# Moving one load to another queue, a block of vector work ahead of another, and eight more zero products, in the pool layer of a two-layer transformer with mixture of experts

## The chip, the cores and the metric

The kernel runs on one core of one Trainium2 chip. The metric is the device time of one execution in microseconds (us), as the median of several runs. One further execution is taken by the hardware profiler; all rows below are of that one execution, with times in us from the start of its span.

## The reference, cut to what matters

Two layers work on 512 tokens of width 1024. The first mixes the tokens by attention, the second by pooling; each is followed by a mixture of experts with 32 experts, of which every token takes two. Before each part the tokens are normed and modulated with a scale and a shift that come from a conditioning vector and the matrix `w_ada` (the modulation). The change lies around the pooling of the second layer:

```python
def pool_mixer(h, w_pool, scale):
    cs = concatenate([0, cumsum(h, axis=1)])
    for gi, win in enumerate((2, 4, 8, 16)):
        lo, hi = maximum(t - win // 2, 0), minimum(t + win // 2, n)
        mean = (cg[:, hi] - cg[:, lo]) / (hi - lo)
        diff = mean - h[..., sl]
        outs.append(diff @ w_pool[gi])
    return concatenate(outs, axis=-1) * scale

x = x + g_m * pool_mixer(modulate(rms_norm(x), sh_m, sc_m))
tokens = modulate(rms_norm(x), sh_f, sc_f)
x = x + g_f * hierarchical_moe(tokens, router weights, w_gate_up, w_down)
```

The router takes a softmax over four groups and the best two of the eight experts in the best group.

## The kernel before, in words

**Weights.** All large weights go through one stream: `plan_stream` lists them in the order of use, `Stream.fill` (the load itself is L136) issues loads on SyncE's queue while fewer than `limit` tiles are out, and `Stream.done` is called when a tile has been used and refills. In the expert layers twelve tiles of 1 MB are out (`RING`). One pair of experts takes eight tiles of gate/up and four of down weights, twelve in all. The last pair's tiles of layer 1 come as two loads of 512 KB each, and so do the gate/up tiles of the first pair of layer 2. Between the layers eight tiles of modulation weights (`ada(1, 2)`, 1 MB each) stand in the stream: in order down weights of pair 15, eight modulation tiles, gate/up weights of the next layer's pair 0. Loads on one queue are issued in the order of the program.

**The experts.** `moe` runs over 16 pairs. For each it multiplies gate and up weights (`up`), adds the previous pair's results (`combine`), gathers the tokens of the next group (`gather`, every second pair works on the same group of four experts), and multiplies the down weights. At the pairs 13 and 14 it takes a step of `late`, a generator that prepares what the next layer needs: `prepare_pool` loads router and pool weights at the first step and scales them at the second. The gathers read a one-hot matrix `OH`, a tile with one buffer; the last of them in a layer comes in pair 13.

**The last pair and the pool layer.** `last_down` multiplies the down weights in two halves of 512 columns. Each half goes through `y`: VectorE gates the product, ScalarE writes the rounded part of `y` (L1410), VectorE the rest (L1450), then TensorE scatters it (`pc`, L1456), VectorE adds it to `x` (L1459) and ScalarE squares the sum (L1460). Between the products of the second half and its `y`, `gap` is called: `pool_begin`. It allocates a new `OH` tile, whose space is used for the banded matrices (`bands`), loads these on ScalarE's queue (L1672), and multiplies the first two modulation tiles (L371). `pool_layer` multiplies four more modulation tiles on TensorE, makes the normed tokens `xn` (L1659, L1661), transposes them (L1700), and treats the eight chunks of 128 columns in two ways: chunks 4 to 7 (windows 8 and 16) by products with the bands (`means`, L1742), chunks 0 to 3 by shifted sums on VectorE (`summed`, L1722 to L1732). The last two modulation tiles stand between (`ada_parts(2)`). `project` multiplies the pool weights (L1759) into the banks g, u, t and y, `added` adds the result to `x` (L1771) and squares it (L1774). `router` multiplies the router weights with the modulation (L1141, L1147) and reads the result with VectorE (L1150 to L1154). `turn` transposes `x` (L1784), `logits` multiplies the router (L1791), and `choose` finds the experts on VectorE (L1181 to L1235). Meanwhile TensorE multiplies zeros into the four banks of the next gather (`zeros`, L1341); these products also clear the banks. Then come `rank` (L1244), the gather itself (L1349) and the second expert layer.

On every engine the instructions run in the order of the program.

Of the kernel before, what the change touches and what calls it, by code (L numbers as in the profile page):

```python
# [11 lines left out]
F32 = mybir.dt.float32  # L12
F32R = mybir.dt.float32r
# [10 lines left out]
NT = SEQ // 128  # L24
# [11 lines left out]
NPAIR = NE // 2  # L36
NWR = (KD - 1) * (NG + NE) + 128

CAP = 56
# [27 lines left out]
_C = {}  # L67
# [129 lines left out]
class Kernel:  # L197
# [1365 lines left out]
    def moe(self, i, late, first, then=lambda: None, later=iter(()), gap=lambda: None):  # L1563

        nc, st = self.nc, self.st
        gf = self.fw[:, 0]
        xe, OH = {0: first}, {}

        def gather(g, k):

            if k == 0:
                xe[g] = self.slots_tile()
            self.gather(i, k, OH[g], 4 * CAP, xe[g][:, k, :4 * CAP])

        self.overflow(i, gf)
        early = self.slots()
        st.fill(RING + 2)
        hold, comb = {}, []

        def up_weights(p, k):  # L1580
            if p in ENDS:
                t = st.get()
                return t[:, 0], t[:, 1]
            if k % 2 == 0:
                hold[0] = [st.get(), st.get()]
            return hold[0][0][:, k % 2], hold[0][1][:, k % 2]

        def down_weights(k):
            if k % 2 == 0:
                hold[0] = [st.get(), st.get()]  # L1590
            return hold[0][0][:, k % 2], hold[0][1][:, k % 2]

        def used(p, k):
            if p == 0:
                next(early, None)
                if k in (4, 6):
                    next(later, None)
            if p in ENDS:
                st.done()
            elif k % 2:  # L1600
                st.done(2)


        st.limit -= 2
        for p in range(NPAIR):
            g = p // 2
            if p % 2 == 0 and p + 2 < NPAIR:
                OH[g + 1] = self.one_hot(g + 1)
            act = self.up(lambda k: xe[g][:, k], [(p % 2 * 2 + e) * CAP for e in range(2)], lambda k: up_weights(p, k), after=lambda k: used(p, k))
            for _ in early:  # L1610
                pass

            turns = [lambda k=k: gather(g + 1, k) for k in range(p % 2 * 4, p % 2 * 4 + 4)] if g + 1 < NPAIR // 2 else []
            for n in range(3):
                for unit in comb[2 * n:2 * n + 2]:
                    unit()
                if turns:
                    turns.pop(0)()
            if turns:
                for unit in comb[6:]:  # L1620
                    unit()
            aT = self.turn_act(act)
            for unit in turns or comb[6:]:
                unit()
            if p in (NPAIR - 3, NPAIR - 2):
                next(late, None)
            w, inv = self.sw[:, p:p + 1], self.sinv[:, p:p + 1]
            if p == NPAIR - 1:

                nc.scalar.activation(self.sm.tile([128, 1], F32, name="warm", bufs=1), self.rk[:, 0, 0:1], AF.Sqrt)  # L1630
                return self.last_down(aT, w, gf, inv, then, gap)
            y = self.down(aT, down_weights, w, gf, lambda k: k % 2 and st.done(2))
            P = self.scatter(inv)
            comb = [unit for h in range(2) for unit in self.combine(P, y[h], h)]


    def prepare_pool(self):

        nc, a = self.nc, self.a
        gw = self.gw = self.big([128, 2, D], F32, "gw")  # L1640
        pw = self.pw = self.big([128, 8, 256], F32, "pw")
        nc.sync.dma_start(gw[:, 1, :NWR], a["w_router"][1])
        self.row_load("pool_scale", lambda h: gw[32 * h:32 * h + 1, 0, :512])
        nc.sync.dma_start(pw, a["pool_w"].rearrange("g (k p) n -> p (g k) n", p=128))
        yield
        for h in range(2):
            row = self.gates[32 * h:32 * h + 1]
            nc.gpsimd.tensor_tensor(row, row, gw[32 * h:32 * h + 1, 0, :512], op=ALU.mult)
        self.row_bcast(self.bank, 2, gw[:, 0])
        for g in range(4):  # L1650
            nc.gpsimd.tensor_tensor(pw[:, 2 * g:2 * g + 2], pw[:, 2 * g:2 * g + 2],
                                    gw[:, 0, None, g * 256:(g + 1) * 256].to_broadcast([128, 2, 256]), op=ALU.mult)

    def scaled(self, norms, outs):

        nc = self.nc
        for j, r in norms:
            if j % 2:
                nc.scalar.activation(outs[j], self.x(j), AF.Copy, scale=r)  # L1659
            else:  # L1660
                nc.vector.tensor_scalar(outs[j], self.x(j), r, 0.0, op0=ALU.mult, op1=ALU.add)  # L1661
# [5 lines left out]

    def pool_begin(self):

        self.bands = self.mp.tile([128, NT, 4 * CAP], F32R, name="OH").rearrange("p a b -> p (a b)").bitcast(F32)  # L1670
        a, b = _C["band"]
        self.nc.scalar.dma_start(self.bands[:, :b - a], self.a["consts"][:, a:b])  # L1672
        self.ada_begin(self.pm, 1, 2, "ga")
        self.ada_parts(2)

    def pool_layer(self, norms):
        nc, mp, pm, st, sm, pw = self.nc, self.mp, self.pm, self.st, self.sm, self.pw
# [39 lines left out]
        def summed(k):  # L1717

            eng = nc.vector
            g = k // 2  # L1720
            h, c, other = (ab[k][:, z] for z in range(3))
            eng.tensor_tensor(c[:, 1:], h[:, 1:], h[:, :-1], op=ALU.add)  # L1722
            w, lo, hi = 2, 1, SEQ + 2 * PAD
            while w < WINDOWS[g]:
                o = w // 2
                eng.tensor_tensor(other[:, lo + o:hi - o], c[:, lo:hi - 2 * o], c[:, lo + 2 * o:hi], op=ALU.add)
                c, other, w, lo, hi = other, c, 2 * w, lo + o, hi - o
            for e, t0 in ((0, PAD), (8, PAD + SEQ - 8)):
                eng.tensor_tensor(c[:, t0:t0 + 8], c[:, t0:t0 + 8], self.edge[:, 16 * g + e:16 * g + e + 8], op=ALU.mult)
            q = slice(PAD, PAD + SEQ)  # L1730
            diff[k] = other[:, q]
            eng.scalar_tensor_tensor(diff[k], c[:, q], 1.0 / WINDOWS[g], h[:, q], op0=ALU.mult, op1=ALU.subtract)  # L1732
# [19 lines left out]
        def project(g, tags):  # L1752

            ps = []
            for jj in range(2):
                p = pm.tile([128, 2, 256], F32, tag=tags[jj], name="pp")
                for j in range(2):
                    for z in range(2):
                        nc.tensor.matmul(p[:, j], diff[2 * g + z][:, (2 * jj + j) * 128:(2 * jj + j + 1) * 128],  # L1759
                                         pw[:, 2 * g + z], start=(z == 0), stop=(z == 1))  # L1760
                ps.append(p)
            return g, ps
# [3 lines left out]
        def added(g, ps):  # L1766

            q = slice(g * 256, (g + 1) * 256)
            for jj in range(2):
                xs = self.xt[jj][:, :, q]  # L1770
                nc.vector.tensor_add(xs, xs, ps[jj])  # L1771
                for j in (2 * jj, 2 * jj + 1):
                    junk = mp.tile([128, 256], F32, name="act")
                    nc.scalar.activation(junk, self.x(j)[:, q], AF.Square, accum_out=ss[:, j, g:g + 1])  # L1774
# [46 lines left out]
        padded(3)  # L1821
        added(*p0)
        p3 = project(3, ("g", "u"))
        self.router(1, self.gw[:, 1])
        self.norm_begin()
        nc.tensor.matmul(self.lg, *zero, start=True, stop=False)
        summed(2)
        summed(3)
        p2 = project(2, ("t", "y"))
        added(*p3)  # L1830
        turn(0, "c", nc.scalar)
# [37 lines left out]
            high(j)  # L1869
        self.banks = {}  # L1870
        for k, tag in ((0, "g"), (2, "u"), (4, "c"), (6, "c")):
            self.zeros(k, tag, 3)
        self.rank(range(NT))
        OH = mp.tile([128, NT, 4 * CAP], F32R, name="OH")
        for j in range(2):
# [81 lines left out]
```

## Time and profile before

| what | value |
|---|---|
| median of the runs | 1393.6 us (1393.39 to 1394.07, three runs) |
| the profiled execution: its time | 1395.2 us |
| its span, first to last instruction | 1393.4 us |
| its mean granted TensorE clock | 0.981 |
| TensorE busy over the span | 95% |
| bytes read from HBM | 472.51 MB, 341 GB/s over the span |

How to read it: engines are PE (TensorE), DVE (VectorE), ACT (ScalarE), POOL (GpSimd) and SP (SyncE). A "q" behind the name is the engine's sequencer, which waits and issues loads. "out<-in" names the tile written and the tiles read. In square brackets stands how long the engine was idle before the instruction and what ended most of that; with a wait for several things it is the one that came last by the profile. Rows of the timeline merge equal instructions that follow each other. The granted clock is 1.00 at 2.4 GHz and 0.50 at 1.2 GHz.

### The profile page before, as it was taken

To read this page: it belongs to the slowest core of one execution; us is meant where nothing else is said; L and a number is where in the kernel's file an instruction comes from. 1 tells how busy PE (TensorE), PEld (TensorE's weight loads), DVE (VectorE), ACT (ScalarE), POOL (GpSimd) and SP (SyncE) were. 2 spreads that over 40 slices of the span, in tenths; PEclk is the share of its full clock that TensorE was granted. 3 is DMA by queue.
4 is the path that set the end of the run, shared out by engine and by line. 5 is a ranking of instruction groups with operands and counts; after the bars stand their busy time and mean duration, and the time that the engine had idled before them with its cause. 6 is when DMAs were issued, how large, how long until landed. Compare 5 with 4: busy or idle time off the path is not lost. (4 is left out here: it accounts for less than half of the span.)

```text
span 1393.4 us, 18658 instructions
## 1 busy us (share of the span) xinstructions
PE 1318.3 (95%) x7179; PEld 738.4 (53%) x7183; DVE 659.7 (47%) x1290; ACT 364.1 (26%) x707; POOL 130.8 (9%) x130
## 2 busy tenths in 40 slices
PE   4799999999899999999999996989999999999995
PEld 1578677778645444554445433854445544454442
DVE  2778788767814343343334334552433433343325
ACT  2554687763311110111111114521101111111103
POOL 0523343340000000000000100000000000000001
PEclk8799999999999999999999998999999999999998
DMA  9411836159499999999999999259999999999994
GB/s 374 164 61 61 343 141 212 52 197 388 195 363 427 426 427 425 427 427 426 427 426 427 414 411 410 118 221 407 426 426 427 426 426 427 426 426 426 427 420 179
DMA packets 80704, 475.91 MB, mean 342 GB/s; under 512 B 8512, under 2 KB 10064, under 8 KB 30432
## 3 DMA queue, kind: packets, MB, share of 16 engines
q1 hardware_dynamic: 80456, 474.22, 83.0%
q8 instruction: 58, 0.95, 0.3%
q10 hardware_dynamic: 152, 0.42, 0.1%
q14 instruction: 38, 0.31, 0.1%
HBM read 472.51 MB, written 2.11 MB: 341 GB/s over the span
## 5 line engine op out<-in xcount | busy, mean ns | idle before, releaser
L1371 PE MATMUL pgate<-wt,xe 128*64 128x512 f32 x1024 | 272.7, 593 | 3.5 <-ACTq L1504 2.1
L1371 PE MATMUL pup<-wt,xe 128*64 128x512 f32 x1024 | 271.3, 592 | 0.3 <-DVEq L1504 0.3
L1396 PE MATMUL py<-wt,aT 128*64 128x512 f32 x960 | 212.6, 595 | 0.0
L1376 DVE TENSOR_TENSOR act<-act,pup 128x512 f32<-128x512 f32 x32 | 22.0, 688 | 343.7 <-ACT act L1375 309.8
L1427 DVE TENSOR_TENSOR x<-x,pc 128x512 f32<-128x512 f32 x240 | 153.9, 683 | 29.9 <-PE pc L1425 29.9
L1371 PEld LDWEIGHTS pgate<-wt,xe 128*64 128x64 f32 x1024 | 75.8, 137 | 149.0 <-issue 128.5
L1371 PEld LDWEIGHTS pup<-wt,xe 128*64 128x64 f32 x1024 | 76.7, 137 | 145.0 <-issue 142.1
L1425 PE MATMUL pc<-y,scat 128*128 128x512 f32 x480 | 136.6, 406 | 2.3 <-DVE x L1427 2.3
L1409 DVE SCALAR_TENSOR_TENSOR py<-py,r_sw,gw 128x512 f32<-128x512 f32 x64 | 48.5, 758 | 178.4 <-PE py L1396 169.5
L1396 PEld LDWEIGHTS py<-wt,aT 128*64 128x64 f32 x960 | 66.9, 137 | 124.0 <-issue 118.8
L1325 PE MATMUL pga<-OH,xnp 128*128 128x224 f32 x896 | 119.3, 277 | 0.0
L1325 PEld LDWEIGHTS pga<-OH,xnp 128*128 128x128 f32 x896 | 114.3, 191 | 8.5 <-issue 1.6
L1375 ACT ACTIVATE act<-pgate 128x512 f32<-128x512 f32 x32 | 19.1, 597 | 361.5 <-PE pgate L1371 349.3
L1425 PEld LDWEIGHTS pc<-y,scat 128*128 128x128 f32 x480 | 80.3, 189 | 42.8 <-ACT act L1375 24.3
L1410 ACT ACTIVATE y<-py 128x512 fp32r<-128x512 f32 x64 | 38.2, 597 | 247.4 <-PE py L1396 182.0
L1334 POOL MEMSET xe<- 128x64 f32 x16 | 2.4, 152 | 785.0 <-PE pup L1371 610.0
L1360 ACT ACTIVATE xe<-pga,mod 128x224 f32<-128x224 f32 x64 | 33.9, 539 | 156.4 <-PE pga L1325 137.2
L562 PE MATMUL pmm<-whl,hT 128*128 128x512 f32 x288 | 70.3, 401 | 0.0
L850 DVE TENSOR_REDUCE mx<-S 128x1 f32<-128x768 f32 x64 | 58.2, 951 | 19.6 <-PE S L847 18.9
L562 PEld LDWEIGHTS pmm<-whl,hT 128*128 128x128 f32 x288 | 54.3, 192 | 11.3
L857 ACT ACTIVATE P<-S,mx 128x768 f32<-128x768 f32 x64 | 57.0, 900 | 2.2 <-POOL rest L731 2.1
L867 PE MATMUL PT<-cst,P 128*128 128x128 f32 x384 | 54.5, 278 | 0.1
(344 smaller groups left out, 1420.9 us busy)
## 6 DMA issues: line engine op xcount, KB each, us to landing
wt<-in_moe_w_gate_up_dram SPq DMA_DIRECT2D x224, 1024.0 KB
wt<-in_moe_w_down_dram SPq DMA_DIRECT2D x120, 1024.0 KB
wt<-in_w_ada_dram SPq DMA_DIRECT2D x48, 1024.0 KB
wt<-in_moe_w_gate_up_dram SPq DMA_DIRECT2D x64, 512.0 KB
wt<-in_moe_w_down_dram SPq DMA_DIRECT2D x16, 512.0 KB
wt<-in_attn_w_qkv_dram SPq DMA_DIRECT2D x6, 1024.0 KB
x<-in_x_dram SPq DMA_DIRECT2D x8, 512.0 KB
wt<-in_attn_w_o_dram SPq DMA_DIRECT2D x4, 1024.0 KB
```

The lines of the kernel that those rows point to most:

```text
L562: self.nc.tensor.matmul(p, lhs(pa, k), whl[pb, k // 4][:, k % 4], start=(k + n == 0), stop=(k == KD - 1 and n == 2))
L850: nc.vector.tensor_reduce(m, s[:, :NKEY], axis=AX, op=ALU.max, negate=True)
L857: nc.scalar.activation(P[n][:, g], S.pop((n, g))[:, :NKEY], AF.Exp, bias=mx[n, g], accum_out=total[n // 4][:, 2 * gp + g, kvl:kvl + 1])
L867: nc.tensor.transpose(pt[:, cc, g * 128:(g + 1) * 128], P[n][:, g, c * 128:(c + 1) * 128], self.ident)
L1325: nc.tensor.matmul(p[:, :n], self.parts[part][j // 2][:, j % 2, k * 128:(k + 1) * 128], OH[:, j], start=(z == 0), stop=(z == 2 * NT - 1))
L1360: nc.scalar.activation(xe, p, AF.Identity, bias=B[:, k:k + 1], scale=A[:, k:k + 1])
L1371: nc.tensor.matmul(p[64 * e:64 * e + 64], xe(k)[:, offs[e]:offs[e] + UNIT], w[e][:, h * 512:(h + 1) * 512], start=(k == 0), stop=(k == KD ...
L1396: nc.tensor.matmul(py[h][64 * e:64 * e + 64], aT[:, j, 64 * e:64 * e + 64], wd[e][:, h * 512:(h + 1) * 512], start=(j == 0), stop=(j == 3) ...
L1409: nc.vector.scalar_tensor_tensor(py, py, w, gf[:, h * 512:(h + 1) * 512], op0=ALU.mult, op1=ALU.mult)
L1410: nc.scalar.activation(y[:, 0], py, AF.Copy)
L1425: nc.tensor.matmul(p, P[:, j * 128:(j + 1) * 128], y[:, part], start=(part == 0), stop=(part == 1))
L1427: nc.vector.tensor_add(xs, xs, p)
```

## The change

Three edits, all between the last pair of experts of layer 1 and the first pair of layer 2.

1. The load of the banded matrices leaves `pool_begin` and ScalarE's queue. It becomes a third step of `prepare_pool`, taken at the start of pair 15, on SyncE's queue. At that point of the program all twelve tiles of pair 15 are listed before it, and the modulation tiles come after it.
2. In `pool_layer` the shifted sums of chunks 2 and 3 stand ahead of the router's work instead of behind it.
3. `zeros` multiplies five products instead of three into each of the four banks.

```diff
@@ moe, in the loop over the pairs
+            if p == NPAIR - 1:
+                next(late, None)
             act = self.up(...)
@@ prepare_pool, at its end
+        yield
+
+        self.bands = self.mp.tile([128, NT, 4 * CAP], F32R, name="OH").rearrange("p a b -> p (a b)").bitcast(F32)
+        u, v = _C["band"]
+        nc.sync.dma_start(self.bands[:, :v - u], a["consts"][:, u:v])
@@ pool_begin
-        self.bands = self.mp.tile([128, NT, 4 * CAP], F32R, name="OH").rearrange("p a b -> p (a b)").bitcast(F32)
-        a, b = _C["band"]
-        self.nc.scalar.dma_start(self.bands[:, :b - a], self.a["consts"][:, a:b])
         self.ada_begin(self.pm, 1, 2, "ga")
         self.ada_parts(2)
@@ pool_layer
         added(*p0)
         p3 = project(3, ("g", "u"))
+        summed(2)
+        summed(3)
         self.router(1, self.gw[:, 1])
         self.norm_begin()
         nc.tensor.matmul(self.lg, *zero, start=True, stop=False)
-        summed(2)
-        summed(3)
         p2 = project(2, ("t", "y"))
@@ pool_layer, after the choice has been issued
-            self.zeros(k, tag, 3)
+            self.zeros(k, tag, 5)
```

## Rows read from the trace of the kernel before

**Rows 1.** The page, the span in 40 equal slices of 34.8 us: GB/s moved

```profile
GB/s 374 164 61 61 343 141 212 52 197 388 195 363 427 426 427 425 427 427 426 427 426 427 414 411 410 118 221 407 426 426 427 426 426 427 426 426 426 427 420 179
```

**Rows 2.** Windows: length, busy us of each engine, granted clock, DMA share, GB/s

```profile
853.00:859.00 6.00, 5.57 (x20) 3.03 (x24) 3.39 (x7) 2.57 (x8) 0.00 (x0) 0.50 1.03 419
885.00:890.00 5.00, 3.42 (x20) 2.90 (x19) 4.81 (x10) 1.69 (x7) 0.00 (x0) 1.00 0.01 3
911.00:914.00 3.00, 3.00 (x16) 3.00 (x16) 3.00 (x7) 0.00 (x0) 0.00 (x0) 0.50 0.03 8
915.00:918.00 3.00, 3.00 (x30) 3.00 (x28) 0.00 (x0) 0.03 (x1) 0.00 (x0) 1.00 0.00 0
925.00:1375.00 450.00, 447.78 (x2278) 213.28 (x2275) 162.73 (x284) 54.18 (x93) 1.06 (x7) 1.00 1.00 418
```

**Rows 3.** Timeline of ScalarE: start, length, instruction, idle before and its releaser

```profile
834.57 0.60 ACT L1410 ACTIVATE y<-py 128x512 fp32r<-128x512 f32 x1 [3.43 <-DVE py L1409]
...
840.32 0.19 ACT L1460 ACTIVATION_READ_ACCUMULATOR act<-x 128x1 f32 x1
852.17 0.36 ACTq L1672 DMA_DIRECT2D OH<-in_consts_dram  x1
852.78 0.60 ACT L1410 ACTIVATE y<-py 128x512 fp32r<-128x512 f32 x1 [12.28 <-DMA wt<-in_moe_w_gate_up_dram]
...
860.27 1.13 ACT L1659 ACTIVATE xn<-x,nr 128x1024 f32<-128x1024 f32 x1
```

**Rows 4.** Timeline of TensorE, 835 to 868

```profile
835.32 2.13 PE L1456 MATMUL pc<-y,scat 128*128 128x512 f32 x8
...
839.24 1.92 PE L371 MATMUL ada_ps<-wt,cond 128*32 128x512 f32 x16
...
853.43 3.78 PE L1456 MATMUL pc<-y,scat 128*128 128x512 f32 x8 [12.26 <-ACT y L1410]
...
861.82 2.17 PE L1700 MATMUL pt<-cst,xn 128*128 128x128 f32 x16
...
866.26 1.92 PE L371 MATMUL ada_ps<-wt,cond 128*32 128x512 f32 x16
```

**Rows 5.** Loads of L136 on SyncE's queue: count, ns to issue, first and last start; timeline

```profile
L136 SPq DMA_DIRECT2D wt<-in_w_ada_dram x8: 327/328/668, 823.6 to 832.6; - x8
...
L136 SPq DMA_DIRECT2D wt<-in_moe_w_gate_up_dram x7: 327/328/328, 835.0 to 849.8; - x7
...
847.30 0.33 SPq L136 DMA_DIRECT2D wt<-in_moe_w_gate_up_dram  x1
```

**Rows 6.** Readers of the tile `OH`, 760 to 870: ns each, first and last start

```profile
L1325 PE MATMUL pga<-OH,xnp x32: 266/274/352, 762.4 to 769.1; 128*128 128x224 f32 x32
...
L1742 PE MATMUL pm<-OH,xn x23: 276/279/286, 864.0 to 869.9; 128*128 128x143 f32 x8, 128*128 128x135 f32 x8, 128*128 128x136 f32 x4, 128*128 128x132 f32 x2
```

**Rows 7.** Timeline of VectorE, 877 to 890

```profile
877.79 1.27 DVE L1771 TENSOR_TENSOR x<-x,pp 128x512 f32<-128x512 f32 x2
882.09 0.17 DVE L1150 COPY mod<-pb 128x16 f32<-128x16 f32 x1 [3.03 <-PE pb L1147]
...
882.65 0.72 DVE L1722 TENSOR_TENSOR pab<-pab 128x543 f32<-128x543 f32 x1
...
887.45 2.47 DVE L1771 TENSOR_TENSOR x<-x,pp 128x512 f32<-128x512 f32 x4
```

**Rows 8.** Timeline of TensorE, 885 to 890

```profile
885.66 1.04 PE L1784 MATMUL pb<-cst,x 128*128 128x128 f32 x8
888.27 1.97 PE L1759 MATMUL pp<-pw,pab 128*128 128x256 f32 x8 [1.58 <-DVE x L1771]
```

**Rows 9.** Timeline of TensorE, 902 to 920

```profile
903.50 2.57 PE L1341 MATMUL pga<-ones_b,tri_b 128*128 128x512 bf16 x11
908.89 0.18 PE L1244 MATMUL pr<-r_M,tri_b 128*128 128x32 bf16 x1 [2.82 <-DVE r_M L1235]
...
910.19 9.08 PE L1349 MATMUL pga<-OH,xnp 128*128 128x224 f32 x64 [0.27 <-DVE OH L1553]
```

## The prediction

> **What bounds the kernel now.** I read the page's 40 slices first. In most slices the weights flow at 426 or 427 GB/s; around the pool layer (slices 25 to 27) they fall to 410, 118 and 221 [rows 1]. The twelve weight tiles that may be out are loaded there and the queue has nothing to do until the second expert layer frees one. What the pool layer takes is therefore paid in full. Behind it TensorE is busy 447.8 of 450 us while the weights run at 418 GB/s [rows 2]: both are full there, but both start from the same event, the first product of the second expert layer, so whatever the pool layer gives back shifts that stretch as a whole.
>
> Next the timeline engine by engine. ScalarE ends its squares at 840.32 + 0.19 = 840.51 and does nothing until 852.17, when it issues the bands' load; at 852.78 comes `y`, which the profile marks as idle 12.28 us for a gate/up weight [rows 3]. TensorE waits 12.26 us for that `y` [rows 4]. This is the largest hole behind the first layer's weights.
>
> Why did ScalarE wait? Look at the weights' queue, in order of issue [rows 5]. The eight modulation tiles of 1 MB leave between 823.6 and 832.6, one per 1.29 us: the pace at which 512 KB halves, like the eight just before them, land at 426 GB/s (1.23 us). The gate/up halves that follow leave one per 2.46 us (seven from 835.0 to 849.8), the pace of 1 MB tiles. So a load leaves when the one eight places ahead has landed. The next place falls at 849.8 + 2.4 = 852.2, and there stands ScalarE's load. It waited for the last modulation tile to land, though it needs none of it, and `y` (L1410), queued behind it, waited too.
>
> **1. The bands' load on SyncE's queue.** Removed: that wait. Added: one load, whose place is taken behind the last pair's weights, ahead of the modulation tiles. Its destination was last read at 769.1 [rows 6], some 54 us before, so the queue does not stand still for it; it is issued at about 823.6 and is there around 834, 30 us before the first band product at 864.0 [rows 6]. Price: 406 KB at 426 GB/s, an estimate of 0.98 us, by which every later tile lands later. Nothing behind it notices except those eight tiles.
>
> What is late next? `y` can start at 840.5. From there:
> - The products `pc` start at about 841.3 (0.75 us behind `y`, as 835.32 stands behind 834.57 in the first half [rows 3, 4]) and take 2.13 us as there, not 3.78, because without the hole the clock stays up; now it is granted 0.50 (1.2 GHz) from 853 to 859 [rows 2]: 843.4.
> - TensorE then multiplies modulation tiles 3 to 6, 0.96 us each (1.92 for two) [rows 4]. The sixth lands now when the load eight places on leaves, at 847.30 [rows 5]; plus 0.98 is 848.28. So they end at about 849.25, and the transposes start then instead of at 861.82 [rows 4]: 12.57 us earlier.
> - The other path, the norm, is ready by then: from `y` at 852.78 to the end of `xn` at 860.27 + 1.13 it takes 8.62 us now [rows 3], products at the low clock included, so it ends at 849.1 at the latest.
> - The last modulation tile lands at 852.17 + 0.98 = 853.15, and TensorE comes to it at about 854.6 (now 866.26 + 0.96, less 12.6 [rows 4]): no wait.
> I take **12.6 us**. Bounds: a load that costs nothing gives 13.5, if the norm gains its us at the full clock; one that costs a full place of 2.46 us gives 11.1.
>
> Here a rule of the Trainium skill speaks against the edit. The page DMA: Bandwidth & Descriptors, section "Issuing engines are not separate DMA queues", says that loads started by different engines run on the same sixteen engines, and that another issuer saves only the time of the issue, which is usually small. By that alone the sum would hold the issue's 0.36 us here instead of 12.6. The trace differs, since what ScalarE loses is not the issue but 11.66 us ahead of it.
>
> **2. Sums of chunks 2 and 3 ahead of the router.** Nothing is added. VectorE ends the sums of group 0 at 877.79 + 1.27 = 879.06, then stands 3.03 us for the router's products (882.09) before it scales the router and, from 882.65 to 887.5, makes the sums of chunks 2 and 3 (4.80 us) [rows 7]. In the new order these run from 879.06 to 883.9, the router's three operations (0.56 us) to 884.4, and the two additions of group 3 (half of 2.47 us) end at 885.7 instead of 888.7. TensorE's `p1` needs these two banks and the sums; it stood 1.58 us for them at 888.27 [rows 8]. TensorE is free after its transposes at 885.66 + 1.04 = 886.70, later than all that. So `p1` starts there: **1.57 us**. The router's operations come 1.8 us later than now; their reader, the logits, comes behind `p1`. Bounds 0 and 3.0 (VectorE's whole advance).
>
> **3. Five zero products for three.** Eight more at 2.57 / 12 = 0.214 us (twelve in the code; the trace holds eleven, spaced 0.22) are 1.7 us: from 906.07 to about 907.8, inside the 2.82 us that TensorE stands for VectorE's choice until 908.89 [rows 9]. In time they cost nothing; without that cover, were the choice as early as 906, they would cost their 1.7 us. What they may give: now TensorE does little from 906.07 to 910.19, and the clock falls; from 911 to 914 it is granted 0.50 (1.2 GHz) and 16 gather products are under way in 3 us, against 30 from 915 to 918 at 1.00 (2.4 GHz) [rows 2]. Those products are spaced 0.21 us instead of 0.11: 16 x 0.1 = 1.6 us and its edges, **1.7 us** of the gather's 9.08 [rows 9]. I take all of it, since the thin stretch shrinks from 4.1 to 2.4 us. Bounds 0 and 1.8.
>
> **Sum.** 12.6 + 1.6 + 1.7 = 15.9 us. The profiled execution took 1395.2 us around a span of 1393.4, so 1379.3 by its own time; the median of the runs is 1.6 lower: **1377.7 us**.
>
> **Rivals.**
> - The clock falls all the same. While TensorE waits for modulation tiles 5 and 6 it works only 0.96 us of each 2.46, the first thin stretch; the one ahead of the gather is the second. For: the fall at 910 after a stretch that wasn't empty. Against: the 1.58 us at 888 did not cost the clock, 1.00 from 885 to 890 [rows 2]. One fall costs 1.7 to 2 us: 1379.5; both 1381.3. Chance 0.24.
> - ScalarE's wait is that of `y` itself: the profile names a weight's DMA as what ended it, and with the load gone `y` waits for the same landing, at 853. Then only the parts 2 and 3 and the issue are left, 1393.6 - 3.3 - 0.4 = 1390. Against: `y` follows the load's issue by 0.6 us without a further stop, and the first half's `y` at 834.57 started right behind VectorE's product [rows 3]. Chance 0.05.
>   The Trainium skill's page DMA: Bandwidth & Descriptors, section "Issuing engines are not separate DMA queues", would give this time too.
> - The load costs more than its bytes, 2.5 to 6 us, and holds the modulation tiles: 1379 to 1383. Chance 0.07.
> - Hidden anyway: the second expert layer is set by its weights' end and the earlier start is lost: 1393.6. Against: the queue idles ahead of it and restarts with it [rows 1]. Chance 0.02.
> - Slower: the weights' queue stands at the bands' load until its tile is free, with all modulation tiles and the next layer's weights behind it. With the load issued at 823.6 + D, the sixth tile lands at 848.3 + D; the gain is gone at D = 16. Were the tile released only by pair 15's last product before the pool layer (841.2), D is 17.6 and the time 1395.3. Against: last read at 769.1 [rows 6]. Chance 0.02.
>
> **The numbers.** The forecast has 0.60, with its own bounds from 13.5 + 3.0 + 1.8 (1375.3) to 11.1 + 1.6 + 1.0 (1379.9). The range takes in the clock rival: 1375.5 to 1381.6; left out are `y`'s own wait, the hidden case, the slower one and the dear end of the costly load, some 0.12, and a little of the forecast's rims. A measurement of this kernel tells about 0.2% (2.8 us) from none. Faster by more: all but the hidden and the slower case, 0.96; within: 0.02; slower: 0.02.
>
> **What would show it.** Right: no wait of TensorE over 2 us between 841 and 850, `y` at about 840.5; the transposes at 849 with the modulation tile as their predecessor; no idle before `p1` and router copies behind the sums; 19 or 20 zero products and a gather near 7.4 us with the clock at 1.00; the expert layer's first product near 904.2. Wrong: `y` still waiting past 845, a hole on SyncE's queue at 823 to 835, or a gather of 9 us.

## The result, and the profile after

The changed kernel takes 1376.82 us in the median (1375.29 to 1378.30, four runs), the kernel before 1393.49 us (1393.23 to 1394.07): a ratio of 0.988 with an interval of 0.9863 to 0.9897. Forecast were 1377.7 us and a range of 1375.5 to 1381.6. The profiled execution took 1378.12 us around a span of 1376.3.

Read it in the order of the prediction. ScalarE, the end of its squares and `y` (start, length, instruction):

```profile
838.06 0.19 ACT L1460 ACTIVATION_READ_ACCUMULATOR act<-x 128x1 f32 x1
838.15 0.58 ACT L1410 ACTIVATE y<-py 128x512 fp32r<-128x512 f32 x1
```

Where [rows 3] had 12.28 us idle, `y` now follows the squares at once. The queue of the weights, SyncE's timeline:

```profile
821.30 0.74 SPq L1659 DMA_DIRECT2D OH<-in_consts_dram  x1
822.70 9.02 SPq L136 DMA_DIRECT2D wt<-in_w_ada_dram  x8
833.87 0.33 SPq L136 DMA_DIRECT2D wt<-in_moe_w_gate_up_dram  x1
```

The bands' load stands right ahead of the eight modulation tiles, and the queue does not stop for it: the next load leaves 1.4 us later. TensorE, in the stretch of [rows 4]:

```profile
836.98 1.92 PE L371 MATMUL ada_ps<-wt,cond 128*32 128x512 f32 x16
838.84 2.13 PE L1456 MATMUL pc<-y,scat 128*128 128x512 f32 x8
840.90 1.92 PE L371 MATMUL ada_ps<-wt,cond 128*32 128x512 f32 x16
843.68 1.06 PE L371 MATMUL ada_ps<-wt,cond 128*32 128x512 f32 x8 [0.86 <-DMA wt<-in_w_ada_dram]
846.11 1.06 PE L371 MATMUL ada_ps<-wt,cond 128*32 128x512 f32 x8 [1.36 <-DMA wt<-in_w_ada_dram]
847.11 1.97 PE L1704 MATMUL pt<-cst,xn 128*128 128x128 f32 x16
```

`pc` takes 2.13 us for 3.78, and a new wait has come in its place: 0.86 and 1.36 us for the fifth and the sixth modulation tile. It is these tiles, not the norm, that now set when the transposes start, though the norm is close behind. VectorE's last part of `xn` ends at 846.85, 0.26 us before the transposes start, and ScalarE's at 847.30, while they run:

```profile
846.09 0.76 DVE L1668 TENSOR_SCALAR xn<-x,nr 128x1024 f32<-128x1024 f32 x1
```

VectorE behind the additions of group 0, which stand in the first row, and TensorE at `p1` (the products of pool weights behind the transposes of L1788; compare [rows 7, 8]):

```profile
862.88 1.28 DVE L1775 TENSOR_TENSOR x<-x,pp 128x512 f32<-128x512 f32 x2
864.07 0.72 DVE L1726 TENSOR_TENSOR pab<-pab 128x543 f32<-128x543 f32 x1
...
868.87 0.17 DVE L1150 COPY mod<-pb 128x16 f32<-128x16 f32 x1
...
869.42 2.48 DVE L1775 TENSOR_TENSOR x<-x,pp 128x512 f32<-128x512 f32 x4
```

```profile
870.74 1.04 PE L1788 MATMUL pb<-cst,x 128*128 128x128 f32 x8
871.62 3.62 PE L1763 MATMUL pp<-pw,pab 128*128 128x256 f32 x16
```

VectorE no longer stands 3.03 us for the router, and `p1` follows the transposes without the 1.58 us of before. TensorE from the zero products to the second expert layer (compare [rows 9]):

```profile
886.56 4.54 PE L1341 MATMUL pga<-ones_b,tri_b 128*128 128x512 bf16 x20
892.14 0.18 PE L1244 MATMUL pr<-r_M,tri_b 128*128 128x32 bf16 x1 [1.05 <-DVE r_M L1235]
...
893.45 7.46 PE L1349 MATMUL pga<-OH,xnp 128*128 128x224 f32 x64 [0.27 <-DVE OH L1553]
901.73 0.65 PE L1371 MATMUL pgate<-wt,xe 128*64 128x512 f32 x2 [0.82 <-ACTq L1504]
```

Windows of the gather and of the second expert layer (length, busy us of each engine, granted clock, DMA share, GB/s; compare [rows 2]):

```profile
894.00:897.00 3.00, 3.00 (x29) 3.00 (x29) 3.00 (x7) 0.00 (x0) 0.00 (x0) 1.00 0.03 8
...
907.00:1357.00 450.00, 447.76 (x2272) 212.93 (x2271) 162.50 (x283) 54.01 (x93) 1.06 (x7) 1.00 1.00 418
```

The clock stayed at 1.00 in the gather, which took 7.46 us for 9.08. The expert layer behind it runs as before, only sooner.

**Where the time came from.** Executions differ by some us far from the edits, so I measure the stretch that the edits touch by itself: the *stage*, from the first modulation product behind the last pair (L371) to the first product of the second expert layer (L1371). It was 839.24 to 920.11 and is 836.98 to 901.73: 80.87 us became 64.75. The whole span fell by 17.07 us; 16.12 of it are the stage, 2.26 were gained ahead of it and 1.30 lost behind it, where nothing was changed.

### The profile page after: what moved, and what is told of

Same layout as the page of the kernel before. It is cut to its first block, busy times and chain, and to the rows that moved or that the text cites. A ratio compares the mean times of both kernels' runs of the same rounds, so it can differ in the third digit from the quotient of the medians.

```text
span 1376.3 us, 18679 instructions
## 1 busy us (share of the span) xinstructions
PE 1314.4 (96%) x7191; PEld 736.4 (54%) x7191; DVE 659.7 (48%) x1290; ACT 363.7 (26%) x707; POOL 130.2 (9%) x130
## 5 line engine op out<-in xcount | busy, mean ns | idle before, releaser
L1371 PE MATMUL pgate<-wt,xe 128*64 128x512 f32 x1024 | 273.1, 593 | 2.7 <-ACTq L1504 2.1
L1371 PE MATMUL pup<-wt,xe 128*64 128x512 f32 x1024 | 271.8, 592 | 0.3 <-DVEq L1504 0.3
L1371 PEld LDWEIGHTS pgate<-wt,xe 128*64 128x64 f32 x1024 | 75.8, 137 | 148.5 <-issue 129.5
L1371 PEld LDWEIGHTS pup<-wt,xe 128*64 128x64 f32 x1024 | 76.5, 137 | 145.5 <-issue 143.2
```

The costliest lines, as they stand in the source:

```text
L1371: nc.tensor.matmul(p[64 * e:64 * e + 64], xe(k)[:, offs[e]:offs[e] + UNIT], w[e][:, h * 512:(h + 1) * 512], start=(k == 0), stop=(k == KD ...
```

## The experiments

The columns are: y, the transposes (L1700 or L1704) and `p1`, each as us behind the first modulation product; the gather's length; the stage; and the median time with its ratio to the kernel before on the same chip. The runs were made on several chips, so that times of different rows are best compared by their ratios.

| kernel | y | transposes | p1 | gather | stage | time, ratio (interval) |
|---|---|---|---|---|---|---|
| before | 13.5 | 22.58 | 49.03 | 9.08 | 80.87 | 1393.5 |
| changed | 1.2 | 10.12 | 34.63 | 7.46 | 64.75 | 1376.8, 0.9880 (0.9863 to 0.9897) |
| edit 1 alone | 1.2 | 10.42 | 36.68 | 9.08 | 68.48 | 1380.0, 0.9903 (0.9889 to 0.9918) |
| edit 2 alone | 14.0 | 22.19 | 47.77 | 9.08 | 79.53 | 1391.4, 0.9986 (0.9977 to 0.9994) |
| edit 3 alone | 13.9 | 22.04 | 49.42 | 9.08 | 81.26 | 1391.1, 0.9979 (0.9970 to 0.9987) |
| load on ScalarE, at pair 15 | 1.2 | 11.31 | 36.30 | 7.46 | 66.42 | 1377.9, 0.9880 (0.9866 to 0.9895) |
| load on SyncE, old place | 1.2 | 9.35 | 49.38 | 7.46 | 79.49 | 1389.7, 0.9972 (0.9960 to 0.9983) |
| load behind the 6th tile | 1.2 | 9.64 | 34.15 | 9.08 | 65.89 | 1378.1, 0.9889 (0.9872 to 0.9905) |
| edits 1 and 2, three zeros | 1.2 | 10.08 | 34.59 | 10.10 | 67.35 | 1380.1, 0.9906 (0.9890 to 0.9923) |
| eight zeros | 1.2 | 10.55 | 35.06 | 7.46 | 66.59 | 1378.6, 0.9898 (0.9881 to 0.9914) |
| changed, again | 1.2 | 10.08 | 34.59 | 7.46 | 64.70 | 1375.4, 0.9881 (0.9865 to 0.9898) |
| six zeros | 1.2 | 10.77 | 35.27 | 7.46 | 65.39 | 1377.7, 0.9894 (0.9877 to 0.9910) |
| six zeros, load behind the 6th tile | 1.2 | 9.20 | 33.91 | 7.45 | 64.02 | 1374.8, 0.9868 (0.9851 to 0.9884) |

Theory: ScalarE stood for the place of its load, eight places ahead in the order of loads; the router's wait held `p1`; the zero products keep the clock up. The main rival: `y` waits for weights by itself.

**Edit 1 alone.** The changed kernel with `summed(2)`, `summed(3)` and the zeros as before:

```diff
-        summed(2)
-        summed(3)
         self.router(1, self.gw[:, 1])
         self.norm_begin()
         nc.tensor.matmul(self.lg, *zero, start=True, stop=False)
+        summed(2)
+        summed(3)
...
-            self.zeros(k, tag, 5)
+            self.zeros(k, tag, 3)
```

> Edit 1 alone: the bands' load on SyncE's queue behind the last pair's weights; the sums stay behind the router and three zero products per bank. The stage is measured from the first modulation product behind the last pair (839.24 in the kernel before) to the first product of the second expert layer (920.11): 80.87 us before, 64.75 us with all three edits. My theory (ScalarE stood for the place of its load, eight places behind): y at the end of the squares, the transposes 12.5 us sooner, the stage 68.4 us, the time 1381 us. Rival (y waits for weights itself, the load's place is not the cause): the stage stays above 80 us and the time above 1392 us.

Measured: `y` 1.2 us behind the first modulation product, transposes 12.2 us sooner, the stage 68.48 us. TensorE's timeline:

```profile
834.18 1.92 PE L371 MATMUL ada_ps<-wt,cond 128*32 128x512 f32 x16
...
843.61 1.07 PE L371 MATMUL ada_ps<-wt,cond 128*32 128x512 f32 x8 [1.36 <-DMA wt<-in_w_ada_dram]
844.60 1.64 PE L1704 MATMUL pt<-cst,xn 128*128 128x128 f32 x13
```

The rival falls: with the load gone nothing else held `y`. The load is the cause, and this edit carries 12.4 of the 16.1 us. It moves the load to another queue and to another place at once; which of the two counts is tried below.

**Edit 2 alone.** `summed(2)` and `summed(3)` ahead of `self.router`, on the kernel before.

> Edit 2 alone: sums of chunks 2 and 3 ahead of the router, on the kernel before. Theory (the 1.58 us before p1 vanish, TensorE is next): the stage 80.87 - 1.6 = 79.2 us, no idle before the products of group 1, the time 1391.9 us. Rival (the router's operations, 1.8 us later, hold a bank or the logits): the stage 80.5 us or more, time unchanged within 0.5 us.

```profile
882.67 1.04 PE L1784 MATMUL pb<-cst,x 128*128 128x128 f32 x8
883.54 3.62 PE L1759 MATMUL pp<-pw,pab 128*128 128x256 f32 x16
```

`p1` comes 0.87 us behind the start of the transposes of L1784, as after the full change (871.62 less 870.74 is 0.88), where it was 2.61 us: 1.74 us, for 1.57 by the forecast. At `p1` the stage had gained only 1.26 us (47.77 for 49.03). The other 0.48 us were lost before, in the hole that this kernel still has: the bands' load left 13.39 us behind the first modulation product (849.16) for 12.93, so that ScalarE's second `xn` (L1659) ended later too. Here it is in this kernel, then in the kernel before:

```profile
858.81 1.15 ACT L1659 ACTIVATE xn<-x,nr 128x1024 f32<-128x1024 f32 x1 [0.40 <-DVE nr L498]
```

```profile
861.80 1.15 ACT L1659 ACTIVATE xn<-x,nr 128x1024 f32<-128x1024 f32 x1 [0.40 <-DVE nr L498]
```

It ends 24.19 us behind the first modulation product for 23.71, and in both kernels the first transposes (L1700) end 1.04 to 1.05 us behind it. So the stage shows 1.3 us.

**Edit 3 alone.** `self.zeros(k, tag, 5)` for 3, on the kernel before.

> Edit 3 alone: five zero products per bank for three, on the kernel before. Theory (they fill TensorE's wait for the choice and keep the clock up): the granted clock of the gather is 1.00, the gather takes 7.4 to 7.5 us for 9.08, the stage 79.2 us, the time 1391.9 us. Rival (the thin stretch ahead of the gather, 2.4 us instead of 4.1, still lets the clock fall): the gather 9 us, the stage 80.9 us, the time as before.

TensorE's timeline, and a window in the gather:

```profile
899.76 4.54 PE L1341 MATMUL pga<-ones_b,tri_b 128*128 128x512 bf16 x20
905.35 0.18 PE L1244 MATMUL pr<-r_M,tri_b 128*128 128x32 bf16 x1 [1.05 <-DVE r_M L1235]
```

```profile
908.50:911.50 3.00, 3.00 (x16) 3.00 (x15) 2.06 (x6) 0.00 (x0) 0.00 (x0) 0.50 0.01 3
```

Here the rival was right in the profiled execution: the products are there, the idle before the rank is 1.05 us as in the changed kernel, and the clock fell all the same, the gather taking 9.08 us. Over its eleven runs the kernel was still faster by 0.2%, as if the clock had stayed up in some of them, which no trace of this kernel shows. So I took it that at five products the clock falls in some executions and not in others, and counted it in what followed.

**The queue or the place?** The changed kernel, issuing the load from ScalarE at the new place:

```diff
-        nc.sync.dma_start(self.bands[:, :v - u], a["consts"][:, u:v])
+        nc.scalar.dma_start(self.bands[:, :v - u], a["consts"][:, u:v])
```

> All three edits, but the load is issued on ScalarE's queue at the same place of the program (start of pair 15). It tells the place from the queue. Theory (what counts is which load stands eight places ahead): ScalarE waits for a half of the last pair's down weights that lands before its own act is due, about 0 to 1 us is lost at that act, the stage is 64.7 us within 1 us, the time within 1.5 us of the changed kernel (1376.8). Rival (any load on ScalarE's queue holds ScalarE until the weights' queue has drained): ScalarE stands 10 us or more somewhere between 800 and 850 and the time is above 1385 us. The rule of the Trainium skill, page DMA: Bandwidth & Descriptors, section 'Issuing engines are not separate DMA queues', by which another issuer only saves the issue, would also have the time of the changed kernel here.

```profile
819.53 0.36 ACTq L1659 DMA_DIRECT2D OH<-in_consts_dram  x1
820.67 0.60 ACT L1375 ACTIVATE act<-pgate 128x512 f32<-128x512 f32 x1 [14.60 <-PE pgate L1371]
```

The load left before ScalarE's next work was due, `act` waited for TensorE alone, and the time is that of the changed kernel (0.9880 of the kernel before, both). The queue is not what cost 12 us. Its stage is 1.7 us longer for other reasons, which TensorE's timeline and a window show:

```profile
845.96 1.93 PE L371 MATMUL ada_ps<-wt,cond 128*32 128x512 f32 x8 [1.36 <-DMA wt<-in_w_ada_dram]
847.82 2.44 PE L1704 MATMUL pt<-cst,xn 128*128 128x128 f32 x16
```

```profile
846.00:848.80 2.80, 2.80 (x13) 1.14 (x14) 0.38 (x1) 0.83 (x1) 0.00 (x0) 0.50 1.00 418
```

The sixth tile's products started 9.45 us behind the first modulation product for 9.13; that is 0.3 us. Then they took 1.93 us for 1.06 at the low clock, and the transposes 2.44 for 1.97; that is 1.3 us. This is the first thin stretch of the prediction's clock rival, met in this one execution.

**The right queue at the old place.** The changed kernel without the new step, and in `pool_begin`:

```diff
-        self.nc.scalar.dma_start(self.bands[:, :b - a], self.a["consts"][:, a:b])
+        self.nc.sync.dma_start(self.bands[:, :b - a], self.a["consts"][:, a:b])
```

> All three edits, but the load stands on SyncE's queue at its old place of the program (pool_begin, behind the next layer's first gate/up halves in the order of issue). Theory (place counts, not the queue): ScalarE's y starts behind its squares as in the changed kernel (1.2 us behind the first modulation product), but the load leaves only when the last modulation tile lands and comes in behind seven or eight halves of 512 KB at 1.23 us, so TensorE stands about 10 us before the first band product; the stage is about 75 us (64.75 with the load early), the time about 1387 us. Rival (it was enough to take the load from ScalarE): no wait before the band products, the stage 64.75 us, the time 1377 us.

SyncE's timeline, then TensorE's:

```profile
852.10 0.33 SPq L1672 DMA_DIRECT2D OH<-in_consts_dram  x1
```

```profile
847.00 2.00 PE L1700 MATMUL pt<-cst,xn 128*128 128x128 f32 x16
861.84 2.23 PE L1742 MATMUL pm<-OH,xn 128*128 128x136 f32 x8 [12.83 <-DMA OH<-in_consts_dram]
```

ScalarE is free, `y` is early, and TensorE waits 12.83 us for the bands: they land 9.7 us behind their issue, since seven halves of 512 KB stand ahead (7 x 1.23 + 0.98 = 9.6). I had the wait at 10 us, mainly because I put the issue at 850 instead of 852.1: the load stands behind all eight halves, the last of which left at 850.86, and so it leaves one place later than ScalarE's did. And the clock fell in the hole (granted 0.50 from 861 to 867), so that the first band products took 2.23 us for 1.12. The stage is 79.49 us. The place is the cause, shown from both sides.

**What the load costs the modulation tiles.** The step is taken behind pair 15's sixth gate/up tile:

```diff
             if p in ENDS:
                 st.done()
+                if p == NPAIR - 1 and k == 5:
+                    next(late, None)
...
-            if p == NPAIR - 1:
-                next(late, None)
```

> All three edits, but the step that issues the load is taken behind the sixth of pair 15's gate/up tiles, so that it stands behind the sixth modulation tile on SyncE's queue instead of ahead of the first. Theory (the load's 0.98 us are paid by the modulation tiles that TensorE waits for): the sixth tile comes 0.98 us sooner, the norm is then nearly as late, the transposes start 0.7 to 0.9 us sooner (9.3 us behind the first modulation product for 10.12), the stage is 64.0 us where the clock stays up, the time 1376 us. Rival (the load costs the tiles nothing, or the norm holds the transposes anyway): the transposes at 10.1 us, the time as the changed kernel's.

```profile
836.38 1.93 PE L371 MATMUL ada_ps<-wt,cond 128*32 128x512 f32 x16
...
845.03 1.06 PE L371 MATMUL ada_ps<-wt,cond 128*32 128x512 f32 x8 [1.38 <-DMA wt<-in_w_ada_dram]
846.02 1.42 PE L1704 MATMUL pt<-cst,xn 128*128 128x128 f32 x11
```

The transposes come 9.64 us behind the first modulation product, and 9.20 in the later kernel with the same place; with the load ahead of all eight tiles at a full clock they came at 10.08 to 10.77, in the mean of six executions at 10.34. The difference of the means is 0.92 us; the load's bytes are 0.98 by the forecast. SyncE's issues of the later gate/up halves show the 0.98 us itself:

```profile
845.05 0.33 SPq L136 DMA_DIRECT2D wt<-in_moe_w_gate_up_dram  x1
846.03 0.33 SPq L136 DMA_DIRECT2D wt<-in_moe_w_gate_up_dram  x1
```

They are the fifth and the sixth gate/up half. In this kernel's order of loads the first stands eight places behind the sixth modulation tile, and it leaves at 845.05 as that tile's products start (845.03, above). The second stands eight places behind the bands' load and leaves 0.98 us later, where the steps around it are 2.5 us. In the changed kernel, whose bands' load stands ahead of all eight tiles, it is the sixth gate/up half that is eight places behind the sixth tile, and that half leaves at 846.08 as the tile's products start (846.11).

The stage did not show the gain, as the clock fell ahead of this execution's gather (9.08 us).

**Fewer and more zero products.** `self.zeros(k, tag, 3)` and then `8` in the changed kernel.

> Edits 1 and 2 without edit 3 (three zero products per bank). Theory: the clock falls ahead of the gather, the gather takes 9.1 us for 7.46, nothing else moves, the stage is 64.75 + 1.6 = 66.4 us, the time 1378.4 us. Rival (the products alone do nothing, since the clock falls or not by chance): the gather is 7.5 us here too.

> All three edits with eight zero products per bank instead of five: twelve more at 0.214 us are 2.6 us, against 1.05 us that TensorE still stood before the rank. Theory (the cover ends at the choice): no idle before the rank, the rank 1.5 us later, the gather 7.46 us at a clock of 1.00, the stage 66.3 us, the time 1378.3 us. Rival (a longer stretch of products gives more back elsewhere, or the rank isn't on the path): the stage 64.8 us or less.

A window of the kernel with three, then the timeline of that with eight:

```profile
891.00:897.00 6.00, 5.36 (x35) 5.20 (x32) 4.74 (x12) 0.00 (x0) 0.00 (x0) 0.50 0.01 4
```

```profile
885.12 6.95 PE L1341 MATMUL pga<-ones_b,tri_b 128*128 128x512 bf16 x31
891.90 0.18 PE L1244 MATMUL pr<-r_M,tri_b 128*128 128x32 bf16 x1
```

With three the clock fell again, as the theory had it, but it stayed low for longer than in the kernel before: from 891 to 897 at least, and the gather took 10.10 us where 9.1 were expected. Why the fall was longer was not tried. With eight there is no idle left before the rank, which comes 57.00 us behind the first modulation product for 55.16. Its `p1` was 0.43 us late, for the modulation tiles, so that 1.4 us are the products': 1.5 were expected. This is the price once the cover is gone.

**The changed kernel again, six products, and both.** `self.zeros(k, tag, 6)`; the last also with the load behind the sixth tile.

> The changed kernel itself once more, for the spread of what lies outside the edits and for the clock ahead of the gather: with five products per bank it has fallen so far in two profiled executions of five, with three in four of four. [...]

> All three edits with six zero products per bank: four more than five per bank, 0.85 us, fit into the 1.05 us that TensorE still stands before the rank. Theory: the idle before the rank falls to 0.2 us, the rank comes no later, the gather is 7.46 us, the stage 64.75 us, the time 0 to 1 us below the changed kernel's on this chip. Rival (the few products between rank and gather let the clock fall anyway): the gather about 9 us, the stage 66.4 us.

> Six zero products per bank and the load behind the sixth modulation tile. Theory: both gains add, the transposes about 9.5 us behind the first modulation product, the gather 7.46 us, the stage 64.2 us, the time about 1 us below the changed kernel's on this chip. Rival (the sixth tile sooner is eaten by the norm, the clock by chance): stage and time as the changed kernel's.

The last kernel, TensorE's timeline:

```profile
835.56 1.92 PE L371 MATMUL ada_ps<-wt,cond 128*32 128x512 f32 x16
...
843.77 1.07 PE L371 MATMUL ada_ps<-wt,cond 128*32 128x512 f32 x8 [1.39 <-DMA wt<-in_w_ada_dram]
844.77 1.50 PE L1704 MATMUL pt<-cst,xn 128*128 128x128 f32 x10
...
890.00 0.18 PE L1244 MATMUL pr<-r_M,tri_b 128*128 128x32 bf16 x1 [0.17 <-DVE r_M L1235]
```

The changed kernel again gives the same stage within 0.05 us. Six products fill the wait, 0.17 us are left of 1.05, and the gather runs at the full clock. That kernel's own time was expected 0 to 1 us below the changed kernel's and is 1377.7 us, against 1375.4 on the same chip; the two intervals overlap. Its stage is 0.69 us longer, because its modulation tiles came late (transposes at 10.77); where the rest comes from was not tried. With both edits the stage is the shortest, 64.02 us, and so is the median, 1374.8 us against 1375.4; their intervals overlap by far, so that I don't call it faster.

Counted over all profiled executions, the clock fell ahead of the gather in four of four with three products per bank, in two of six with five, and in none of three with six or eight. That three products are too few is plain from this; that six are better than five is not, since two of six and none of three can come by chance.

## Why the prediction was right

- **What ScalarE waited for.** The reading of [rows 5], that a load leaves when the one eight places ahead has landed, is borne out by moving the place and the queue apart: the same load from ScalarE at an earlier place holds nothing. That it is the eighth load ahead shows in the kernel with the load behind the sixth tile: the one short step of 0.98 us, among steps of 2.5, comes eight places behind the small load. That ScalarE's load has a place in the same row is read from the times alone: in the kernel before it left 2.38 us behind SyncE's seventh half (849.79), the step of 1 MB, and SyncE's eighth half left 1.24 us behind it (853.41), the step of 512 KB.
- **Edit 1: 12.6 us forecast, 12.46 measured** (transposes from 22.58 to 10.12 behind the first modulation product). The next wait was named rightly, and its time too: the sixth tile's products 9.04 us behind the first by the forecast, 9.13 in the trace. The load's 0.98 us is 0.98 in the queue's issues and 0.92 at the transposes.
- **Edit 2: 1.57 us forecast, 1.94 measured** from the transposes to `p1`. Of it 1.74 stand before `p1`, and 0.20 belong to edit 1, which shows them alone too (26.26 us for 26.45): the transposes took 1.97 us for 2.17. The 1.57 was a little small because I let `p1` start when the transposes of 1.04 us end; it starts 0.88 us behind their start.
- **Edit 3: 1.7 us forecast, 1.62 measured where the clock stays up.** The size was right, the certainty was not: I took the whole of it into the sum although the stretch was only made shorter, and with five products the clock fell in two executions of six. With the clock up in four of six the mean worth is nearer 1.1 us, an estimate.
- **The sum: 15.9 forecast, 16.12 in the stage.** That the stage's gain goes whole into the time held: the kernel's two pairs of medians differ by 16.7 and 16.9 us. The forecast's own bounds were drawn too tight at one end: 1379.9 us takes 1.6 and 1.0 us for edits 2 and 3, whose own lower bounds were 0; with those it would be 1382.5.
- **The rivals.** `y`'s own wait, the hidden gain and the queue that stands for the tile are refuted, the last by the 1.4 us from the load's issue to the next. So is the dear load, which would have cost 2.5 us or more and cost 0.98. The clock rival is real at both of its places: 1.3 us at the first in the one execution that shows it, and 1.6 at the second, or 2.6 in the execution of edits 1 and 2 with three products.

By the section "Issuing engines are not separate DMA queues" of the Trainium skill's page DMA: Bandwidth & Descriptors, another issuer should change nothing but the time of the issue. That is borne out by the load on ScalarE at the new place, 0.9880 of the kernel before as with the load on SyncE. The forecast held this rule against the whole edit, but the edit moves the load's place as well, of which the rule says nothing. What the rule leaves out is the wait of an engine that runs its instructions in order at its own issue, 11.66 us here.

## What to carry to other kernels

A load on a compute engine's queue can hold all work behind it for a landing that it does not need; look in the trace which load stands a fixed number of places ahead, and issue the small load where that one has long landed, whatever the queue. Then ask what else the load's place delays: here eight tiles by its own bytes, on the path. Filling an engine's wait with idle products is free only up to the end of that wait: eight per bank cost 1.4 us here. What they protect has to be counted over several executions, since with five per bank the clock was up in some traces and down in others, in a stretch whose code was the same.

## What the runs showed of the hardware that was not expected

Between executions the same code ahead of the edits moved by more than some edits are worth: the first modulation product stood between 834.2 and 839.2 us in the thirteen profiled executions. In part it is the end of the first expert layer. The turns of `act` (L1383) in the pairs 12 to 15, before and then after:

```profile
L1383 PE MATMUL paT<-cst,act x16: 270/272/273, 738.6 to 828.7; 128*128 128x128 f32 x16
```

```profile
L1383 PE MATMUL paT<-cst,act x16: 270/272/273, 738.3 to 826.4; 128*128 128x128 f32 x16
```

The same three pairs took 90.1 us and 88.1, though no edit comes before the last of them. In the second layer the pairs 12 to 15 took the other way round, 83.9 and 85.2 us. Before those pairs TensorE keeps the same pace to 0.1 us in both. I take it that at the end it has caught up with the weights, so that small differences of their pace show. This is not shown: of the 2.0 us in the first layer, the waits that the profile lays to a gate/up weight explain 1.0 (1.2 us before, 0.2 after), and in the second layer it names none. Why the pace differs was not tried.
